# Attention by head pairs: the first head's queries turned feature-major in the bank of the values

## The chip, the cores and the metric

The kernel runs on one core of one Trainium2 chip. The metric is the device time of one execution in microseconds. The core's engines work at the same time, each on its own fixed list of instructions: TensorE (PE, matrix products and transposes; its weight loads are shown apart as PEld), VectorE (DVE), ScalarE (ACT), GpSimd (POOL) and SyncE (SP, which here issues the transfers). An instruction starts when the one ahead of it on its engine lets it and when the semaphores that it waits for have been raised by other engines or by transfers. PE writes its results to PSUM, which this kernel uses as eight banks of 128 rows by 512 floats; ACT and DVE read them from there.

## The reference

Two residual layers over 512 tokens of 1024 features, each followed by a SwiGLU network. The first layer (a state-space mixer beside a gated linear attention) and the networks are outside this change. The second layer is a latent attention with 16 heads; a head has 64 features without position, 32 rotated ones, and 64 value features:

```python
cq, ckv, k_rope = jnp.split(h @ w_dqkv, [MLA_Q_RANK, MLA_Q_RANK + MLA_KV_RANK], axis=-1)   # 384, 256, 32
q = (rms_norm(cq, q_lora_norm) @ w_uq).reshape(bsz, seqlen, H, MLA_NOPE + MLA_ROPE)
q_nope, q_rope = jnp.split(q, [MLA_NOPE], axis=-1)
kv = (rms_norm(ckv, kv_lora_norm) @ w_ukv).reshape(bsz, seqlen, H, MLA_NOPE + MLA_V)
k_nope, v = jnp.split(kv, [MLA_NOPE], axis=-1)
q_nope = rms_norm(q_nope, q_nope_norm)
q_rope = apply_rope(rms_norm(q_rope, q_rope_norm), cos[:, None, :], sin[:, None, :])
k_nope = rms_norm(k_nope, k_nope_norm)
k_rope = apply_rope(rms_norm(k_rope, k_rope_norm), cos, sin)
...
    s = jnp.einsum('bqhd,bkhd->bhqk', qn, k_nope) + jnp.einsum('bqhr,bkr->bhqk', qr, k_rope)
    s = s.astype(jnp.float32) * scale
    p = jax.nn.softmax(jnp.where(mask, s, -jnp.inf), axis=-1).astype(v.dtype)
    return jnp.einsum('bhqk,bkhv->bqhv', p, v)
...
return o @ w_o
```

## The kernel before

**The products.** Weights and activations are split into a high and a low part, and each product is three matmuls (L180 to L182, one after the other in `mm3`): high by high, low by high, high by low. A weight comes by one transfer on SP (`weight`, two buffers); ACT then casts it to its high part (L170, tile `whi`) and DVE subtracts to get the low part (L171, tile `wlo`). What PE made in PSUM and has to be split goes the same way through `split` (ACT's copy at L140, DVE's subtraction at L141).

**The heads.** The attention works by pairs of heads, p = 0 to 7, and by groups of two pairs, g = 0 to 3. Queries and keys of a group are made token-major by the projections (`queries`, `keys`: tiles `qs`, `ks`, and the values `v`), normalised by DVE (`heads_norm`: sums at L1077; factors, whose chain ends with L203 to L206; the factors are applied at L1098 to the keys, L1099 and L1105 to the queries) and rotated in four steps at L993 to L996, of which L996 writes the rotated queries. Then `prepare` turns one pair feature-major: PE transposes the keys of both heads (four transposes, L1127), ACT and DVE (L1141) copy them to `kT`; PE transposes the queries of the first head (four, L1148), ACT copies them to `qT` (L1153); and the same for the second head. L1141 and L1153 carry the gains of the norms, so they are needed anyway.

**A pair's steps.** A pair has three steps (query blocks 0 and 1, block 2, block 3). In each PE makes the scores of both heads (L1181, tile `sco`), DVE masks them and takes the maximum (L1192), ACT the exponential (L1194), DVE the reciprocal (L1196) and the normalisation (L1198); PE transposes the result (L1209, tile `ptr`), and ACT copies it to `pt` (L1218). When all three are there, PE makes the values of both heads (L1228, tile `po`), which `split` turns into operands of the last product (`o_round`, 512 columns at a time).

**The banks.** Of the eight banks, three are the pool `acc`, which hands them out in rotation to all projections, to the transposes of the keys and to those of the queries. The other five belong to this phase by name; `aux(tag)` asks for one:

```python
open_phase(sco=2, ptr=2, po=1, st="sco")
```

A tile that asks for a bank waits until the last reader of its former tile is done. So before the change the bank `po` is used once for each pair, by its values, from the first of their matmuls to the subtraction of `split`.

**The order.** One loop runs over the 24 steps and two more. In step s it emits the values of the pair before (in the second step of a pair), the transposes of the last step's scores, the scores of the next step, and then the pieces that a table, `plan`, gives to that step: projections and norms of later groups, `get_ready(p + 1)`, which is `prepare` for the next pair (in a pair's second step), and the first half of the output product. The order in which the instructions are emitted is not yet the order on the engines. A scheduler puts them there by priority (the order of emission, moved ahead by 90 places for weights and by 150 for some copies), by their data, by a few orders written out by hand, and by its model of when a bank is free. A tile that takes another bank can thus move other instructions on all engines.

Of the kernel before, what the change touches and what calls it, by code (L numbers as in the profile page):

```python
# [46 lines left out]
def kernel(ctx: ExitStack, tc: tile.TileContext, A, yT, stop=99):  # L47
# [11 lines left out]
    def nm(s):  # L59
        cnt[0] += 1  # L60
        return f"{s}_{cnt[0]}"

    def acc():
        return pacc.tile([P, T], F32, tag="acc", name=nm("acc"))
# [11 lines left out]
    def aux(tag="st"):  # L76
        while isinstance(phase["tags"][tag], str):
            tag = phase["tags"][tag]
        return phase["p"].tile([P, T], F32, tag=tag, name=nm(tag), bufs=phase["tags"][tag])
# [19 lines left out]
    ps = acc()  # L99
# [3 lines left out]
    def col(name, i=0, lo=0, hi=P):  # L103
        j = PV[name] + i
        return pv[lo:hi, j:j + 1]
# [18 lines left out]
    def order(i, behind, reason):  # L124

        tc.add_manual_dep(i.ins, behind.ins.name,
                          mybir.DependencyInfo(mybir.DependencyClass.NoSync, mybir.DependencyReason.DATA),
                          reason=reason)
# [229 lines left out]
    with tc.tile_pool(name="gkp", bufs=1) as gkp:  # L358

        ps = aux("a1")  # L360
# [72 lines left out]
        with tc.tile_pool(name="ssd", bufs=2) as sp:  # L433
            cw = sp.tile([P, 60], F32, name="cw", bufs=1)
            j = PV["conv_w"]
# [245 lines left out]
        with tc.tile_pool(name="gla", bufs=2) as gp:  # L681
# [17 lines left out]
            for h in range(4):  # L699
                ps = aux()  # L700
# [209 lines left out]
    with tc.tile_pool(name="mla", bufs=2) as mp, tc.tile_pool(name="mla1", bufs=1) as m1:  # L910
# [30 lines left out]
        ps = acc()  # L941
# [56 lines left out]
        ps = aux()  # L998
# [122 lines left out]
        def prepare(g, hp, mms=None):  # L1121


            qs, ks = pr[g][:2]
            ps = acc()
            for i in range(4):
                tr = E.transpose(ps[:, i * P:(i + 1) * P],  # L1127
                                 ks[:, i, 2 * hp:2 * hp + 2, :].rearrange("p h d -> p (h d)"), ident)
                if mms is not None:
                    order(tr, mms[2][-1], "keys behind products that run until they are normalised")  # L1130
            if mms is not None:
                order(mms[3][0], tr, "the last products behind the keys")
            kts, qts = [], []
            for j in range(2):
                t = kT[(4 * g + 2 * hp + j) % NK]
                kts.append(t)
                with tc.high_priority(offset=FREE):
                    if j == 0 and mms is None:
                        S.activation(t[0:64, :], ps[0:64, :], AF.Copy, scale=col("k_gain", 0, 0, 64))
                    else:  # L1140
                        done = V.tensor_scalar(t[0:64, :], ps[64 * j:64 * j + 64, :],  # L1141
                                               col("k_gain", 0, 64 * j, 64 * j + 64), None, ALU.mult)
            if mms is not None:
                keys.first = done
            for j in range(2):
                ps = acc()
                for i in range(4):
                    tr = E.transpose(ps[0:96, i * P:(i + 1) * P], qs[:, i, 2 * hp + j, :], ident)  # L1148
                    if mms is not None:
                        order(tr, mms[3][0], "queries behind products that run until they are rotated")  # L1150
                qT = mp.tile([96, T], F32, tag="qT", name=nm("qT"), bufs=4)
                with tc.high_priority(offset=FREE):
                    i = S.activation(qT, ps[0:96, :], AF.Copy, scale=col("q_gain", 0, 0, 96))  # L1153
                qts.append(qT)
            if mms is not None:
                order(mms[3][1], tr, "the very last product behind the queries")
                order(keys.last, i, "the last keys behind the first queries")
            return kts, qts
# [107 lines left out]
        ps = aux()  # L1266
# [23 lines left out]
        mms = list(keys(1, wk1))  # L1290
        ahead = [None] * 9
        ahead[0] = prepare(0, 0, mms)
        a0 = apply(0, 1, rq, rk)

# [7 lines left out]
        def get_ready(p):  # L1302
            ahead[p] = prepare(p // 2, p % 2)
            yield
# [132 lines left out]
```

## Time and profile before

| | |
|---|---|
| Median of 3 runs | 1340.86 us (1340.81 to 1341.13) |
| Profiled execution | 1340.57 us |
| Span of its trace | 1338.3 us |
| PE busy between 790 and 965 us, where the pairs are worked off | 173.14 of 175 us |
| DVE busy there | 142.12 us |
| ACT busy there | 131.57 us |
| PE busy in 650 to 790 us, ahead of it | 139.94 of 140 us |
| PE busy in 965 to 1338 us, behind it | 369.46 of 373 us |

The span is the time from the first to the last instruction in the trace; the execution's own time holds a little more on both sides. A busy time is the sum of an engine's instructions without overlap; matmuls are pipelined, so on PE the distance from the start of one row to the start of the next says more than the lengths. The pairs' scores, transposes and values fill the stretch from about 790 to 965 us, with the projections of later pairs and the first half of the output product between them. There PE, DVE and ACT are all near their limits, while ahead of it and behind it PE alone is.

### The profile page before, as it was taken

What the parts mean: (1) busy time and instruction counts of PE and PEld (TensorE: products, weight loads), DVE (VectorE), ACT (ScalarE), POOL (GpSimd) and SP (SyncE); (2) the same over time, 40 slices, a digit from 0 to 9 for tenths busy, and PEclk for the clock granted to TensorE, in tenths of its full rate; (3) what the DMA queues carried; (4) which work ended last, traced back from release to release, by engine and by line L of the source; (5) the groups of instructions that cost most, each with busy time, mean ns of one, the idle gap of its engine ahead of it and who ended that gap; (6) DMA issues with size and microseconds to landing.
All of it is one profiled execution on the core that took longest, in us unless ns stands there. A gap on an engine that the chain in (4) does not pass through costs nothing.

```text
span 1338.3 us, 16696 instructions
## 1 busy us (share of the span) xinstructions
PE 1330.8 (99%) x6508; PEld 1092.8 (82%) x6508; DVE 813.3 (61%) x1389; ACT 561.8 (42%) x956; POOL 7.8 (1%) x35
## 2 busy tenths in 40 slices
PE   9999999999999999999999999999999999999998
PEld 6888888888888888888888888777788888888887
DVE  7889967778976444444333469997674444443221
ACT  7675625444353333222222348986543222232210
POOL 0000000000000000000000000000000000000000
PEclk9999999999999999999999999999999999999999
DMA  5442232312233233333333321110123333333331
GB/s 181 127 142 85 90 95 82 95 63 64 90 97 97 95 95 95 95 96 100 92 102 102 97 92 51 48 32 33 64 95 95 95 96 102 101 95 95 114 112 58
DMA packets 36927, 122.23 MB, mean 91 GB/s; under 512 B 4785, under 2 KB 5809, under 8 KB 36849
## 3 DMA queue, kind: packets, MB, share of 16 engines
q1 hardware_dynamic: 36032, 120.72, 29.2%
q8 instruction: 51, 0.84, 0.3%
q10 hardware_dynamic: 816, 0.46, 0.1%
q14 instruction: 28, 0.22, 0.1%
HBM read 119.03 MB, written 2.13 MB: 91 GB/s over the span
## 4 chain that ended last, share of the span: by engine, by line
PE 92%; DVE 5%; ACT 2%; issue 1%; DMA 1%; SPq 0%; POOL 0%; POOLq 0%; DVEq 0%; ACTq 0%
PE acc L180 28%; PE acc L181 28%; PE acc L182 28%; PE sco L1181 2%; PE po L1228 1%; PE ptr L1209 1%; DVE sc L1192 1%; DVE wlo L171 1%; PE a L570 1%; PE a L810 1%; DVE sc L1198 1%; DVE st L1077 0%; PE a L561 0%; PE a L815 0%; PE a L539 0%
## 5 line engine op out<-in xcount | busy, mean ns | idle before, releaser
L170 ACT CAST whi<-wraw 128x1024 fp32r<-128x1024 f32 (+2 forms) x217 | 223.4, 1030 | 561.6 <-PE acc L181 425.0
L180 PE MATMUL acc<-xh,whi 128*128 128x512 f32 x1144 | 449.8, 393 | 0.2 <-ACT qT L1153 0.2
L181 PE MATMUL acc<-xl,whi 128*128 128x512 f32 x1144 | 446.1, 390 | 0.0
L182 PE MATMUL acc<-xh,wlo 128*128 128x512 f32 x1144 | 445.8, 390 | 0.0
L171 DVE TENSOR_TENSOR wlo<-wraw,whi 128x1024 fp32r<-128x1024 f32 (+2 forms) x217 | 259.2, 1195 | 143.2 <-ACT whi L170 142.7
L180 PEld LDWEIGHTS acc<-xh,whi 128*128 128x128 f32 x1144 | 214.8, 188 | 45.4 <-issue 0.8
L182 PEld LDWEIGHTS acc<-xh,wlo 128*128 128x128 f32 x1144 | 214.8, 188 | 44.5
L181 PEld LDWEIGHTS acc<-xl,whi 128*128 128x128 f32 x1144 | 214.9, 188 | 44.3 <-issue 0.4
L880 DVE TENSOR_TENSOR fu<-acc,R 128x512 f32<-128x512 f32 x44 | 30.4, 691 | 137.4 <-PE acc L182 137.4
L182 PE MATMUL acc<-fhh,wlo 128*128 128x512 f32 x288 | 112.0, 389 | 0.0
L180 PE MATMUL acc<-fhh,whi 128*128 128x512 f32 x288 | 112.0, 389 | 0.0
L181 PE MATMUL acc<-fhl,whi 128*128 128x512 f32 x288 | 112.0, 389 | 0.0
L877 DVE TENSOR_TENSOR fg<-acc,R 128x512 f32<-128x512 f32 x44 | 30.4, 691 | 89.3 <-PE acc L182 89.3
L180 PEld LDWEIGHTS acc<-fhh,whi 128*128 128x128 f32 x288 | 54.1, 188 | 11.3
L182 PEld LDWEIGHTS acc<-fhh,wlo 128*128 128x128 f32 x288 | 54.1, 188 | 11.3
L181 PEld LDWEIGHTS acc<-fhl,whi 128*128 128x128 f32 x288 | 54.1, 188 | 11.1
L180 PE MATMUL acc<-mxh,whi 128*128 128x512 f32 x128 | 49.8, 392 | 0.0
L181 PE MATMUL acc<-mxl,whi 128*128 128x512 f32 x128 | 49.7, 389 | 0.0
L182 PE MATMUL acc<-mxh,wlo 128*128 128x512 f32 x128 | 49.7, 389 | 0.0
L1194 ACT ACTIVATE sc<-sc,mx 128x128 f32<-128x128 f32 (+3 forms) x64 | 35.5, 558 | 12.5 <-DVE mx L1192 12.2
L1181 PE MATMUL sco<-kT,qT 96*128 96x256 f32 (+3 forms) x128 | 39.3, 438 | 0.1
L894 DVE TENSOR_TENSOR x<-x,acc 128x512 f32<-128x512 f32 x16 | 11.0, 688 | 42.9 <-PE acc L182 42.9
(375 smaller groups left out, 1602.3 us busy)
## 6 DMA issues: line engine op xcount, KB each, us to landing
wraw<-in_w_gate_dram SPq DMA_DIRECT2D x44, 512.0 KB, 3.5
wraw<-in_w_up_dram SPq DMA_DIRECT2D x44, 512.0 KB, 3.5
wraw<-in_w_down_dram SPq DMA_DIRECT2D x32, 512.0 KB, 3.6
wraw<-in_w_out_dram SPq DMA_DIRECT2D x16, 512.0 KB, 3.5
wraw<-in_w_down_dram SPq DMA_DIRECT2D x16, 384.0 KB, 3.1
wraw<-in_w_xbc_dram SPq DMA_DIRECT2D x11, 512.0 KB, 3.6
wraw<-in_w_z_dram SPq DMA_DIRECT2D x8, 512.0 KB, 3.5
wraw<-in_w_v_dram SPq DMA_DIRECT2D x8, 512.0 KB, 3.5
```

Of the source, the lines that this page charges most:

```text
L170: cast = S.copy(hi[:, :kc * m], r)
L171: i = V.tensor_tensor(lo[:, :kc * m], r, hi.bitcast(F32)[:, :kc * m], ALU.subtract)
L180: E.matmul(out, ah, bh, start=first, stop=False)
L181: E.matmul(out, ah, bl, start=False, stop=False)
L182: return E.matmul(out, al, bh, start=False, stop=last)
L570: i = E.matmul(pd[64 * h:64 * h + 64, c * P:(c + 1) * P], xdt[:, c, h, :], mt[:, h, c, :], start=True, stop=True)
L810: i = E.matmul(po[e][:, r * P:(r + 1) * P], v[:, r, e * P:(e + 1) * P], sc[:, r, :], start=True, stop=(r == 0))
L877: V.tensor_tensor(g, pg, R, ALU.mult)
L880: V.tensor_tensor(u, pu, R, ALU.mult)
L1181: i = E.matmul(ps[:, at:at + n], self.qts[j][:, b * P:(b + 1) * P], self.kts[j][:, :n], start=True, stop=True)
L1192: V.tensor_tensor_reduce(sc[:, at:at + n], ps[:, at:at + n], am[:, T - n:], -scale, 3e38, ALU.add, ALU.min, mx[:, j:j + 1])
L1194: S.activation(sc[:, at:at + n], sc[:, at:at + n], AF.Exp, bias=mx[:, j:j + 1], scale=-1.0, accum_out=sm[:, j:j + 1])
```

## The change

The first head's four query transposes go to the bank `po`, those of the second head stay in the rotation of `acc`:

```diff
@@ -1143,7 +1143,8 @@ def prepare(g, hp, mms=None):
             for j in range(2):
-                ps = acc()
+
+                ps = acc() if j else aux("po")
                 for i in range(4):
                     tr = E.transpose(ps[0:96, i * P:(i + 1) * P], qs[:, i, 2 * hp + j, :], ident)
```

The file gets one line longer there, so everything behind it is found one line later: L1148 becomes L1149, L1153 L1154, L1181 L1182, L1192 L1193, L1196 L1197, L1198 L1199, L1209 L1210, L1228 L1229. No instruction is added or left out. From the first pair on the scheduler lays the three engines out differently; SP and POOL keep their order. The rows below are an engine's instructions in order: line, operation, result and operands by tile name and number, shape, and how many in a row.

At the third pair (p = 2), PE's list around the transposes of its keys (`ks_6748`) and queries (`qs_6636`) was this. `ptr_7163` and `ptr_7168` are the transposed scores of a step of the pair before, `ptr_7212` of the step after it, `sco_7175` the new pair's first scores:

```order
L1127 MATMUL acc_7142<-ident,ks_6748 128x128 x4
L1209 MATMUL ptr_7163<-ident,sc_7032 128x128 x3
L1209 MATMUL ptr_7168<-ident,sc_7035 128x128 x3
L1148 MATMUL acc_7149<-ident,qs_6636 96x128 x4
L1148 MATMUL acc_7156<-ident,qs_6636 96x128 x4
L1209 MATMUL ptr_7212<-ident,sc_7113 128x128 x4
L1181 MATMUL sco_7175<-kT_6606,qT_7154 128x128
L1181 MATMUL sco_7175<-kT_6606,qT_7154 128x256
```

The second head's score transposes `ptr_7218` stood later, behind a product of six matmuls (`acc_7203`). With the change the same place reads:

```order
L1210 MATMUL ptr_7163<-ident,sc_7032 128x128
L1127 MATMUL acc_7142<-ident,ks_6748 128x128 x4
L1210 MATMUL ptr_7163<-ident,sc_7032 128x128 x2
L1210 MATMUL ptr_7168<-ident,sc_7035 128x128 x3
L1210 MATMUL ptr_7212<-ident,sc_7113 128x128 x4
L1210 MATMUL ptr_7218<-ident,sc_7116 128x128 x4
L1149 MATMUL po_7149<-ident,qs_6636 96x128 x4
L1149 MATMUL acc_7156<-ident,qs_6636 96x128 x4
L180 MATMUL acc_7203<-whi_7062,lh_6455 128x512
L181 MATMUL acc_7203<-wlo_7063,lh_6455 128x512
L1182 MATMUL sco_7175<-kT_6606,qT_7154 128x128
```

Both heads' score transposes moved ahead of the query transposes, and the first two matmuls of the product moved in front of the scores.

On DVE at the same pair, before, with `rt_7128` a half of the rotation of `qs_6636` that L996 adds in, and `kT_6608` the copy of the second head's keys:

```order
L995 TENSOR_TENSOR qs_6636<-rr_7126,csq 128x4x2x32
L1098 TENSOR_TENSOR ks_6748<-ks_6748,hry_7047 128x4x128
L1196 RECIPROCAL sm_7118<-sm_7118 128x2
L996 TENSOR_TENSOR qs_6636<-qs_6636,rt_7128 128x4x2x32
L1198 TENSOR_SCALAR sc_7113<-sc_7113,sm_7118 128x512
L1198 TENSOR_SCALAR sc_7116<-sc_7116,sm_7118 128x512
L1141 TENSOR_SCALAR kT_6608<-acc_7142,pv 64x512
L1099 TENSOR_TENSOR qs_6636<-qs_6636,hry_7047 128x4x2x64
L1105 TENSOR_TENSOR rr_7239<-qs_6636,hry_7047 128x256
```

And with the change:

```order
L1098 TENSOR_TENSOR ks_6748<-ks_6748,hry_7047 128x4x128
L1141 TENSOR_SCALAR kT_6608<-acc_7142,pv 64x512
L1197 RECIPROCAL sm_7118<-sm_7118 128x2
L993 TENSOR_TENSOR rt_7128<-rr_7126,csq 128x8x16
L1199 TENSOR_SCALAR sc_7113<-sc_7113,sm_7118 128x512
L1199 TENSOR_SCALAR sc_7116<-sc_7116,sm_7118 128x512
L994 TENSOR_TENSOR rt_7128<-rr_7126,csq 128x8x16
L995 TENSOR_TENSOR qs_6636<-rr_7126,csq 128x4x2x32
L1099 TENSOR_TENSOR qs_6636<-qs_6636,hry_7047 128x4x2x64
L996 TENSOR_TENSOR qs_6636<-qs_6636,rt_7128 128x4x2x32
```

The key copy, the two normalisations and the L1099 of the pair after now stand ahead of the rotation's last step L996, and the first steps L993 and L994 are pulled apart. A little ahead of it, in the factors of this group (`hry_7047`) and just ahead of the split of the second pair's values, stands a subtraction for a weight that before came 18 rows behind L996:

```order
L203 SCALAR_TENSOR_TENSOR hry_7047<-hrt_7048,hry_7047 128x48
L204 TENSOR_TENSOR hrt_7048<-hry_7047 128x48
L171 TENSOR_TENSOR wlo_7463<-wraw_7460,whi_7462 128x1024
L205 SCALAR_TENSOR_TENSOR hrt_7048<-st_6637,hrt_7048 128x48
L141 TENSOR_TENSOR xl_1269_7096<-po_7086,xh_1268_7095 128x512
L206 SCALAR_TENSOR_TENSOR hry_7047<-hrt_7048,hry_7047 128x48
```

It is the row of `wlo_7463` that moved; the others keep their order.

At the fifth pair (p = 4), PE's list before, with `acc_7549` and `acc_7556` the transposed queries of the two heads:

```order
L1127 MATMUL acc_7542<-ident,ks_7066 128x128 x4
L1148 MATMUL acc_7549<-ident,qs_6852 96x128 x4
L1209 MATMUL ptr_7563<-ident,sc_7432 128x128 x2
L1148 MATMUL acc_7556<-ident,qs_6852 96x128 x4
L1209 MATMUL ptr_7563<-ident,sc_7432 128x128
L1209 MATMUL ptr_7568<-ident,sc_7435 128x128 x3
L1181 MATMUL sco_7575<-kT_6606,qT_7554 128x128
```

With the change:

```order
L1127 MATMUL acc_7542<-ident,ks_7066 128x128 x4
L1149 MATMUL po_7549<-ident,qs_6852 96x128 x4
L1149 MATMUL acc_7556<-ident,qs_6852 96x128 x4
L1210 MATMUL ptr_7563<-ident,sc_7432 128x128 x3
L1210 MATMUL ptr_7568<-ident,sc_7435 128x128 x3
L180 MATMUL acc_7610<-whi_7462,lh_6455 128x512
L1182 MATMUL sco_7575<-kT_6606,qT_7554 128x128
```

The eight query transposes now stand together, directly behind the keys', and a first product matmul stands ahead of the scores. At the second pair the eight query transposes moved ahead of five of six score transposes, and the scores now follow them directly. At the sixth pair the output product `acc_7725` now stands directly behind the query transposes, and the score transposes behind it. At the first pair a matmul of the next queries' product moved ahead of the scores.

## The prediction

> **What bounds the kernel now.** I read the engine totals first, then what TensorE (PE) waits for over the whole span, then the stretches in which the change lies.
>
> ```profile
> PE 1330.8 (99%) x6508; PEld 1092.8 (82%) x6508; DVE 813.3 (61%) x1389; ACT 561.8 (42%) x956; POOL 7.8 (1%) x35
> ...
> PE acc L101 <- DVE idle L98: 1.3, 1, 1.3
> PE acc L1148 <- DVE kT L1141: 0.6, 1, 0.6
> PE acc L1148 <- DVE qs L996: 0.5, 1, 0.5
> PE acc L1148 <- ACT v L1062: 0.4, 1, 0.4
> PE acc L180 <- ACT qT L1153: 0.2, 1, 0.2
> ...
> 800.00:850.00 50.00, 48.94 (x263) 39.50 (x262) 44.33 (x141) 43.73 (x105) 1.73 (x3) 1.00 0.18 58
> 850.00:900.00 50.00, 49.20 (x283) 36.55 (x282) 46.61 (x151) 43.15 (x114) 0.00 (x0) 1.00 0.13 43
> ```
>
> PE is busy for 1330.8 of 1338.3 us: it is the bound, and only 7.5 us of idle time are left in all, most of them at the two ends. The waits (microseconds in total, times, longest) name what can be won in the attention: four short waits of PE, three of them at the query transposes of L1148. Two of these, and the one of L180, are waits for an accumulator bank or can be such; the one for L996 is a wait for data, the rotated queries. The windows (length, then busy time of PE, weight loads, VectorE (DVE), ScalarE (ACT), POOL, then the granted clock) say what stands close behind PE there: between 800 and 900 us DVE is busy 44.3 and 46.6 of 50 us, ACT 43.7 and 43.2. So in this stretch an operation that DVE does earlier makes another one later.
>
> **The gaps that can go.** The PE timeline of before (start, length, line, tile; in brackets the idle time and its releaser) shows them as steps from start to start that are longer than elsewhere. Rows of one place follow each other directly, except that some at 820 and 896 us have other work behind them.
>
> ```profile
> 820.62 0.60 PE L1148 MATMUL acc<-ident,qs 128*96 128x128 f32 x4
> 821.77 0.61 PE L1148 MATMUL acc<-ident,qs 128*96 128x128 f32 x4 [0.56 <-DVE kT L1141]
> ...
> 832.82 0.82 PE L1209 MATMUL ptr<-ident,sc 128*128 128x128 f32 x6
> 834.13 1.08 PE L1148 MATMUL acc<-ident,qs 128*96 128x128 f32 x8 [0.50 <-DVE qs L996]
> ...
> 849.70 0.82 PE L1209 MATMUL ptr<-ident,sc 128*128 128x128 f32 x6
> 850.67 1.08 PE L1148 MATMUL acc<-ident,qs 128*96 128x128 f32 x8
> 851.58 0.60 PE L1209 MATMUL ptr<-ident,sc 128*128 128x128 f32 x4
> 852.08 1.58 PE L1181 MATMUL sco<-kT,qT 96*128 96x128 f32 x8
> ...
> 854.90 0.60 PE L1209 MATMUL ptr<-ident,sc 128*128 128x128 f32 x4
> 855.33 1.46 PE L1181 MATMUL sco<-kT,qT 96*128 96x384 f32 x4
> ...
> 866.62 1.04 PE L1148 MATMUL acc<-ident,qs 128*96 128x128 f32 x8
> 867.50 0.82 PE L1209 MATMUL ptr<-ident,sc 128*128 128x128 f32 x6
> 868.16 1.58 PE L1181 MATMUL sco<-kT,qT 96*128 96x128 f32 x8
> ...
> 883.22 0.38 PE L1209 MATMUL ptr<-ident,sc 128*128 128x128 f32 x2
> 883.96 0.64 PE L1148 MATMUL acc<-ident,qs 128*96 128x128 f32 x4 [0.35 <-ACT v L1062]
> ...
> 896.22 0.82 PE L1209 MATMUL ptr<-ident,sc 128*128 128x128 f32 x6
> 897.27 0.50 PE L180 MATMUL acc<-xh,whi 128*128 128x512 f32 x1 [0.24 <-ACT qT L1153]
> ```
>
> The place at 866 us runs without a wait and gives the measure: eight query transposes take 0.88 us (866.62 to 867.50), so four take 0.44; six score transposes take 0.66, so two take 0.22. Against it the gaps are: (a) at 820 us 1.15 - 0.44 = 0.71; (b) at 832 us 1.31 - 0.66 = 0.65; (c) at 849 us 0.97 - 0.66 = 0.31; (d) at 883 us 0.74 - 0.22 = 0.52; (e) at 896 us 1.05 - 0.66 = 0.39. Sum 2.58 us. This is the most that the change can win if nothing is put in place of them: 0.19% of the time.
>
> **The change part by part.** It adds and removes no operation, no transfer and no byte; DMA issues, SP and POOL keep their order. It takes the first head's four transposes and the copy that reads them (L1153) out of the rotation of the three acc banks and into the po bank. Two kinds of effect follow.
>
> *The bank itself.* The first head's transposes no longer wait for an acc bank but for the split of the values that were in po before, whose last reader is DVE's L141; and each pair's values wait for the copy of the queries. The nearest case of the first in before:
>
> ```profile
> 893.93 0.68 DVE L141 TENSOR_TENSOR xl<-po,xh 128x512 fp32r<-128x512 f32 x1
> ...
> 895.35 1.04 PE L1148 MATMUL acc<-ident,qs 128*96 128x128 f32 x8
> ```
>
> The split ends at 894.61, 0.74 us ahead of the transposes. I cost this new wait at nothing: its cover is the score transposes, scores and key transposes between values and queries, all on PE. If DVE reached the split 1 us later, 0.3 us would show there. Queued behind a waiting transpose on PE is everything, so such a wait would be paid in full. The other way round, the values stand 5 us or more behind the queries' copies. Nothing.
>
> *The order.* With other banks free at other times, the scheduler lays out all three engines anew from the first pair to the fifth; this is the larger part. At (a) the second head's transposes get a bank that ACT has long emptied: the 0.71 goes. At (b) DVE now has the rotation two rows earlier and the 1.12 us split of weights behind it: that wait goes too, though the scores then stand right behind the transposes and wait for ACT's copies, which I put at about the same size.
>
> The third pair (849 to 855 us) decides. There the score transposes of the step before (ptr_7212 and ptr_7218, eight) now stand ahead of the query transposes, and on DVE five operations that stood behind the rotation of these queries (the first L996 shown) stand ahead of it: the weight split wlo_7463, the key copy kT_6608, two normalisations L1198, and a L1099. Their steps in before:
>
> ```profile
> 850.21 0.40 DVE L996 TENSOR_TENSOR qs<-qs,rt 128x256 f32<-128x256 f32 x1
> 850.53 0.88 DVE L1198 TENSOR_SCALAR sc<-sc,sm 128x512 f32<-128x512 f32 x2
> 851.44 0.76 DVE L1141 TENSOR_SCALAR kT<-acc,pv 64x512 f32<-64x512 f32 x1
> 852.23 0.69 DVE L1099 TENSOR_TENSOR qs<-qs,hry 128x512 f32<-128x512 f32 x1
> 852.84 0.42 DVE L1105 TENSOR_TENSOR rr<-qs,hry 128x256 f32<-128x256 f32 x1
> ...
> 855.22 1.21 DVE L171 TENSOR_TENSOR wlo<-wraw,whi 128x1024 fp32r<-128x1024 f32 x1
> 856.34 0.48 DVE L1198 TENSOR_SCALAR sc<-sc,sm 128x128 f32<-128x128 f32 x2
> ```
>
> From start to start: 0.91 for the two normalisations, 0.79 for the key copy, 0.61 for L1099, 1.12 for the weight split: 3.43 us. DVE is full here, so nothing that PE wins at (a) and (b) lets DVE come to this point earlier; the rotation ended at 850.61 and PE's queries began at 850.67, so they now begin near 850.67 + 3.43 = 854.10. Of that wait PE does eight score transposes that it did later in before: 0.50 us (851.58 to 852.08) and 0.43 us (854.90 to 855.33). What is left at the scores of 855.33 is 3.43 - 0.50 - 0.43 = **2.50 us later**, and it holds whatever was won up to there: (a), (b) and (c) are swallowed, since the time of this point is DVE's.
>
> The bounds of this term: nothing, if DVE has enough air from other rows to be back in time; and about 3.1, if the split wlo_7463 has to wait for its cast. The cast is ACT's:
>
> ```profile
> 844.24 1.06 ACT L170 CAST whi<-wraw 128x1024 fp32r<-128x1024 f32 x1
> ...
> 844.84 0.21 DVE L205 SCALAR_TENSOR_TENSOR hrt<-st,hrt 128x48 f32<-128x48 f32 x1
> ```
>
> The split now stands where L205 began at 844.84, and the cast ended at 845.30: up to about 0.5 us of waiting, against some tenths saved because short dependent rows of the factors now have other work between them. I take 2.50, the value nearest to the rows, with no correction.
>
> Behind this point I find no second place of the kind: the later rotations and key copies keep 0.4 us or more in front of PE's need. What is left of the gaps goes: at (d) both heads' transposes find free banks (0.52), at (e) the product that waited for ACT's copy takes a bank emptied long before (0.39). I credit both in full, less nothing: 0.91. Bounds: 0 and 1.1.
>
> **The sum** against the profiled execution: 1340.57 + 2.50 - 0.91 = 1342.16 us (its span is 1338.3, with 2.3 us around it, which stay). The median of the runs of before, 1340.86, stands 0.29 above that execution; so the forecast median is 1342.16 + 0.29 = 1342.45, rounded to **1342.4 us**, 0.12% above. A measurement of this kernel tells about 0.2%, 2.7 us, from no change.
>
> **The rivals.** *The gaps go and nothing takes their place.* For it: DVE's share of 1338 us is only 61%, and if the five operations find air, PE gets all of 2.58: 1340.86 - 2.58 = 1338.3. Against it: DVE's 46.6 of 50 us in just this window, and the rows that follow each other without a break. Even then the change is at the edge of what can be measured. Chance 9%, a third of it beyond 0.2%.
>
> *The banks were not what PE waited for* (the waits named are by the last semaphore), the new order costs and wins little: 1340.9, within half a microsecond. For it: two of the five gaps are waits for data. Against it: the order shown changes anyway. 12%.
>
> *Slower: PE's clock falls at the third pair.* PE would now stand still ahead of ptr_7212: it comes there at about 850.36 - 0.71 = 849.65 and is released when the two normalisations are done, near 852.5, so it idles some 2.8 us, does 0.9 us of work and idles again till 854.1. The longest wait of PE in before is 1.3 us. What PE does after standing still shows only at the start:
>
> ```profile
> 1.32 4.45 PE L101 MATMUL acc<-idle 128*128 128x512 bf16 x10 [1.32 <-DVE idle L98]
> 5.29 0.90 PE L363 MATMUL a<-xh,whi 128*48 128x512 f32 x1
> ...
> 7.54 0.40 PE L363 MATMUL a<-xh,whi 128*48 128x512 f32 x1
> 7.77 0.39 PE L364 MATMUL a<-xh,wlo 128*48 128x512 f32 x1
> ```
>
> The first ten matmuls of 512 columns took (5.29 - 1.32) / 10 = 0.40 us each, later ones 0.23 from start to start: 1.7 us lost on ten, and I add 0.6, a third of it, for those behind them, the first of which is still 0.90 long. Priced like that the time is 1342.4 + 2.3 = 1344.7. It decides from the point where the idle stretch is long enough; the granted clock in the windows (1.00 throughout) has no such stretch to show it by. Chance 13%. [...]
>
> *The values' split is late in each pair.* If DVE came to L141 a microsecond late behind its other rows, seven pairs would pay a few tenths each, 2 us on top: 1344.4. Against it: in the order the split stands ahead of the score rows as before. 4%.
>
> **How the numbers follow.** The forecast has what is left, 62%; its own range, by the bounds of its two terms (0 to 3.1 and 0 to 1.1, not both at their ends), is 1340.6 to 1343.8, and a tenth of it lies above 1343.5. The range that should hold 8 times in 10 reaches down over the case of the banks and part of the way to that of the gaps, and up to the clock: 1339.4 to 1344.8. Faster by over 0.2% (below 1338.2): 0.03. Slower (above 1343.5): 0.06 of the forecast, 0.13 and 0.04: 0.23. Within 0.2%: 0.74.
>
> **What the profile of the changed kernel would show.** If I am right, PE has a new wait of 2 to 3 us near 849 to 852 us at the score transposes L1210, released by DVE's normalisation L1199, and a second one below 1 us at the query transposes L1149, released by L996; the waits for kT and for v at the query transposes are gone, and none of po's transposes waits for L141. PE's idle time in 800 to 900 us rises from 1.9 us to about 4. Wrong would be: the queries of the third pair beginning before 852 us (the order then costs less than its rows say), waits of over 1 us at any other pair, or matmuls of 0.4 us from start to start behind 854 us.

## The result and the profile after

The changed kernel takes 1342.81 us (median of 20 runs, 1341.65 to 1344.28) against 1340.89 us of the kernel before (20 runs, 1340.27 to 1342.91 and a single one of 1471.93): 1.92 us more, a ratio of 1.0014 with a 95% interval of 1.0007 to 1.0020. It is slower, since the interval lies above 1, but by less than the 0.2% that the prediction took as its bound. The profiled execution took 1343.48 us, its span is 1341.3 us.

The changed kernel's waits of PE (total, times, longest) and its two windows of 50 us (length; busy PE, weight loads, DVE, ACT, POOL; granted clock; DMA share, GB/s):

```profile
PE ptr L1210 <- DVE sc L1199: 2.9, 1, 2.9
PE acc L101 <- DVE idle L98: 1.3, 1, 1.3
...
800.00:850.00 50.00, 50.00 (x269) 40.60 (x268) 44.26 (x138) 43.12 (x103) 1.73 (x3) 1.00 0.23 75
850.00:900.00 50.00, 47.14 (x266) 35.50 (x264) 44.30 (x146) 41.00 (x109) 0.00 (x0) 0.97 0.10 32
```

The four waits in the attention are gone; the stretch from 800 to 850 us has no idle time left (1.06 us before). In their place stands one wait of 2.9 us behind 850 us, and the granted clock of that window is 0.97, where it was 1.00 in both before.

To see where time was won and lost, the same rows are compared in both traces. The first pair here is the last row ahead of the pairs (L1268 before, L1269 after); then the values of the first, second, third, fourth and fifth pair (L1228 before, L1229 after). First before, then after:

```profile
804.74 0.60 PE L1268 MATMUL sco<-ident,kro 128*32 128x128 f32 x4
...
843.14 2.38 PE L1228 MATMUL po<-pt,v 128*64 128x512 f32 x16
859.87 2.37 PE L1228 MATMUL po<-pt,v 128*64 128x512 f32 x16
876.22 2.37 PE L1228 MATMUL po<-pt,v 128*64 128x512 f32 x16
890.17 2.38 PE L1228 MATMUL po<-pt,v 128*64 128x512 f32 x16
909.18 2.37 PE L1228 MATMUL po<-pt,v 128*64 128x512 f32 x16
```

```profile
805.78 0.60 PE L1269 MATMUL sco<-ident,kro 128*32 128x128 f32 x4
...
842.95 2.38 PE L1229 MATMUL po<-pt,v 128*64 128x512 f32 x16
863.88 2.38 PE L1229 MATMUL po<-pt,v 128*64 128x512 f32 x16
880.35 2.38 PE L1229 MATMUL po<-pt,v 128*64 128x512 f32 x16
893.64 2.37 PE L1229 MATMUL po<-pt,v 128*64 128x512 f32 x16
912.17 2.37 PE L1229 MATMUL po<-pt,v 128*64 128x512 f32 x16
```

The profiled execution of after is already 1.04 us late when it reaches the pairs, at work that the change doesn't touch. That belongs to the executions: after's stands 0.67 us above its kernel's median and before's 0.32 below, 0.99 together. So it is taken off below, and likewise in every kernel of the experiments (-0.19 to 1.20 us at the same row). The differences then are -1.23 us at the first values, +2.97 at the second, +3.09, +2.43 and +1.95 at the next. So 1.23 us were won up to the third pair's preparation, 4.20 lost there, 0.12 more lost at the fourth pair, 0.66 and 0.48 won at the next two. The sum, 1.95 us, agrees with the medians' 1.92.

The loss, on PE and DVE of the changed kernel at the third pair (start, length):

```profile
849.63 0.71 PE L1210 MATMUL ptr<-ident,sc 128*128 128x128 f32 x5
853.19 1.83 PE L1210 MATMUL ptr<-ident,sc 128*128 128x128 f32 x8 [2.86 <-DVE sc L1199]
854.82 1.06 PE L1149 MATMUL po<-ident,qs 128*96 128x128 f32 x4
855.67 1.06 PE L1149 MATMUL acc<-ident,qs 128*96 128x128 f32 x4
856.38 0.64 PE L180 MATMUL acc<-whi,lh 128*128 128x512 f32 x1
```

```profile
845.67 1.22 DVE L171 TENSOR_TENSOR wlo<-wraw,whi 128x1024 fp32r<-128x1024 f32 x1
...
851.12 0.76 DVE L1141 TENSOR_SCALAR kT<-acc,pv 64x512 f32<-64x512 f32 x1
...
852.17 0.88 DVE L1199 TENSOR_SCALAR sc<-sc,sm 128x512 f32<-128x512 f32 x2
...
854.11 0.42 DVE L996 TENSOR_TENSOR qs<-qs,rt 128x256 f32<-128x256 f32 x1
```

PE is out of work at 850.34, and waits for the two normalisations; then its eight score transposes take 1.63 us from start to start (0.20 each, where eight transposes took 0.88 before), the next four 0.85 and the last four 0.71. Windows of one microsecond of the same kernel show why:

```profile
851.00:852.00 1.00, 0.00 (x0) 0.00 (x0) 0.94 (x4) 1.00 (x4) 0.00 (x0) 1.00 0.00 0
852.00:853.00 1.00, 0.00 (x0) 0.00 (x0) 1.00 (x5) 0.13 (x1) 0.00 (x0) 1.00 0.00 0
853.00:854.00 1.00, 0.81 (x5) 0.84 (x6) 1.00 (x4) 0.00 (x0) 0.00 (x0) 0.66 0.00 0
854.00:855.00 1.00, 1.00 (x6) 0.99 (x5) 1.00 (x4) 0.59 (x1) 0.00 (x0) 0.50 0.06 16
855.00:856.00 1.00, 1.00 (x7) 0.95 (x6) 1.00 (x4) 0.67 (x2) 0.00 (x0) 0.50 0.00 0
856.00:857.00 1.00, 1.00 (x6) 0.94 (x5) 1.00 (x3) 0.83 (x2) 0.00 (x0) 0.63 0.00 0
```

The granted clock, the third number from the end of each row, fell to a half when PE had just begun to work again. From these shares (twice 0.34 + 0.50 + 0.50 + 0.37) it was low for 3.42 us.

### The profile page after: what moved, and what is told of

The parts are those of the page before. It is cut to its first block, busy times and chain, and to the rows that moved or that the text cites. A ratio compares the mean times of both kernels' runs of the same rounds, so it can differ in the third digit from the quotient of the medians.

```text
span 1341.3 us, 16692 instructions
## 1 busy us (share of the span) xinstructions
PE 1331.9 (99%) x6508; PEld 1094.5 (82%) x6508; DVE 813.5 (61%) x1389; ACT 562.1 (42%) x956; POOL 7.8 (1%) x35
## 4 chain that ended last, share of the span: by engine, by line
PE 95%; ACT 2%; DVE 2%; issue 1%; DMA 0%; POOL 0%; SPq 0%; POOLq 0%; ACTq 0%
PE acc L180 28%; PE acc L181 28%; PE acc L182 28%; PE sco L1182 2%; PE po L1229 1%; PE ptr L1210 1%; PE a L570 1%; PE a L810 1%; ACT sc L1195 0%; PE a L561 0%; PE a L815 0%; PE a L539 0%; DMA x<-in_xT_dram 0%; DVE wlo L171 0%; ACT whi L170 0%
## 5 line engine op out<-in xcount | busy, mean ns | idle before, releaser
L1182 PE MATMUL sco<-kT,qT 96*128 96x256 f32 (+3 forms) x128 | 39.1, 438 | 0.0
```

What stands on the lines that cost most here:

```text
L1182: i = E.matmul(ps[:, at:at + n], self.qts[j][:, b * P:(b + 1) * P], self.kts[j][:, :n], start=True, stop=True)
```

## The experiments

The theory: the bank itself costs nothing; the loss is DVE's rows that now stand ahead of the rotation, the wait of PE that follows, and the clock's fall after that wait. The rivals: the hand-over of the bank po costs something at every pair; the slow matmuls have another cause; the gaps that went come back elsewhere. Each kernel was timed against before on the same chip, with 11 runs of its own and 21 or 33 of before.

**The weight's subtraction back behind the rotation.** The kernel has a list `hold`: a weight's subtraction that is emitted while something stands in it is ordered behind that.

```diff
         def keys(g, wkv=None):
 
+            if g == 3:
+                hold.append(q_done[1, 0])
             wkv = wkv or k_weights(g)
+            hold.clear()
```

> The change, and besides one order by hand: DVE's subtraction of the last keys' weight (wlo_7463), which the change had moved ahead, stays behind the rotation of the third pair's queries. Theory A (the moved rows on DVE and the order on PE that follows from them are the loss; the bank itself costs nothing): the query transposes of the third pair begin at most 0.5 us later than before, PE waits there 1 to 2 us, the granted clock stays 1.000, and the gaps at the other pairs stay closed: 1339.5 to 1340.5 us. Theory B (the hand-over of the bank po is the loss, the order only its form): still 1342.5 or more. Theory C (the change wins nothing anywhere, the gaps come back elsewhere): 1340.9.

Measured: 1340.31 us (1340.02 to 1341.59), ratio 0.9996 (0.9987 to 1.0005). With that one row back, the scheduler also puts the query transposes ahead of the score transposes again. PE at the third pair of this kernel:

```profile
849.08 0.82 PE L1213 MATMUL ptr<-ident,sc 128*128 128x128 f32 x6
851.86 0.64 PE L1152 MATMUL po<-ident,qs 128*96 128x128 f32 x4 [1.97 <-DVE qs L996]
```

This execution was 0.61 us late at the last row ahead of the pairs (805.35), so the queries begin 851.86 - 0.61 - 850.67 = 0.58 us later than before, as against 3.11 with the change (854.82 - 1.04 - 850.67), and slightly more than the 0.5 expected. What PE had won up to here it spends in a wait of 1.97 us, since the rotation on DVE is not earlier. Theory B falls: the bank is used as in the change, and the time is 2.5 us lower. Theory C is not settled by this time alone, since its interval contains 1; the pair of kernels with and without po further down settles it.

**Work for PE in the wait.** Twenty transposes of the unit matrix are put into po ahead of the third pair's queries:

```diff
                 ps = acc() if j else aux("po")
+                if (g, hp, j) == (1, 0, 0):
+                    for _ in range(20):
+                        E.transpose(ps[:, 0:P], ident, ident)
```

> The change, and besides 20 idle transposes of the unit matrix into the third pair's po bank ahead of its queries, 20 x 0.11 = 2.2 us of PE work that lies in the 2.86 us wait; nothing of the result changes. Theory A1 (PE's clock fell because of the wait, and that costs about 1.0 us): the granted clock is 1.000, the eight score transposes take 0.87 us instead of 1.63, the wait before them is about 0.7 us, and the time falls to about 1341.8. Theory A2 (the slow matmuls behind the wait come from something else that stands in this place): they stay at about 0.2 us each and the time stays at 1342.8. Theory A3 (the idle work delays the path): above 1343.

Measured: 1342.11 us (1341.62 to 1343.30), ratio 1.0011 (1.0002 to 1.0020). The PE timeline of this kernel:

```profile
849.80 2.24 PE L1150 MATMUL po<-ident 128*128 128x128 f32 x19
851.87 0.82 PE L1213 MATMUL ptr<-ident,sc 128*128 128x128 f32 x6
853.37 1.06 PE L1213 MATMUL ptr<-ident,sc 128*128 128x128 f32 x8 [0.68 <-ACT pt L1222]
854.75 0.64 PE L1152 MATMUL po<-ident,qs 128*96 128x128 f32 x4 [0.32 <-DVE qs L996]
```

With more work on PE than the change has, the loss is smaller: the score transposes are back at 0.13 us or less each, the granted clock is 1.00 throughout, and the wait for the rotation that I had expected behind them comes out, 0.32 us. (The 0.68 us are named after ACT's copy, which ended at 853.26; DVE's second normalisation had ended at 853.22.) The second pair's values, at 863.06 and with 1.20 us of lateness ahead of the pairs taken off, stand 1.99 us after before's, 0.98 less than with the change. By the medians it is 0.70 us less; the two intervals overlap, so the size rests on the trace.

**The change for some of the pairs.** Once for p = 0 and 1 alone, once for p = 3 to 7:

```diff
-                ps = acc() if j else aux("po")
+                ps = aux("po") if not j and 2 * g + hp < 2 else acc()
```

```diff
-                ps = acc() if j else aux("po")
+                ps = aux("po") if not j and 2 * g + hp >= 3 else acc()
```

> The change for the first two pairs alone, all others in the three acc banks as before. Theory A: the order at the third pair is that of the change though its own queries are not in po, with PE's wait of nearly 3 us and the clock's fall; the gaps at the fifth and sixth pair (0.9 to 1.0 us together) are back: about 1343.8. Theory B (each pair in po costs something): two pairs of eight, 1341.4 at most, and no wait over 1 us at the third pair.

> The change for the last five pairs alone (p = 3 to 7), the first three in acc as before. Theory A: the first three pairs run as before, with their gaps, the third pair as before without the long wait; the gaps at the fifth and sixth pair are gone, 0.9 to 1.0 us: about 1339.9. Theory B: five pairs of eight pay for the bank, 1341.5 to 1342. Theory C (gaps closed there come back behind): 1340.9.

Measured: 1343.78 us (ratio 1.0018, 1.0009 to 1.0027) with the first two pairs, 1340.26 us (0.9994, 0.9986 to 1.0003) with the last five. In the first, the third pair has its queries in acc and still shows `PE ptr L1210 <- DVE sc L1199` with 2.9 us and the clock's fall: the loss at the third pair comes from the order that the first two pairs' banks bring about. The sum of both, +2.89 and -0.63 us against the same runs of before, is +2.26; the whole change has +1.92. The last five pairs win less than the 0.9 to 1.0 us expected, and the interval of their time contains 1; by the trace, the values of the fourth pair stand 0.16 us and those of the fifth 0.66 us earlier than before's. At the fifth pair the gap came back in part as a new wait of 0.40 us of the scores for ACT's copy, as theory C has it.

**The key copy back, the weight's subtraction left where it is.**

```diff
             if mms is not None:
                 keys.first = done
+            if (g, hp) == (1, 0):
+                order(done, q_done[1, 0], "copy of the keys behind the rotation")
```

> The change, and besides one order by hand: DVE's copy of the second head's keys at the third pair (kT_6608, 0.78 us) stays behind the rotation; the weight's subtraction stays where the change put it, and PE's order is that of the change. If each row on DVE counts in full, PE's wait at the score transposes shrinks from 2.86 to about 2.1 us; whether the clock falls after 2.1 us is open: with the fall 1342.0, without it about 1341.0 and a granted clock of 1.000. Rival (the wait is not set by DVE's rows but by PE's own order): wait still 2.9 us and 1342.8.

Measured: 1342.18 us (1340.76 to 1342.92), ratio 1.0007 (0.9998 to 1.0015). The wait is 2.38 us, 0.48 less than with the change, where the full row would have been 0.78. Part of the row's place is taken: a rotation step, L994, now stands ahead of the normalisations with 0.19 us, and their reciprocal waits 0.16 us for ACT's exponential. The 11 runs fall into two groups by the mean granted clock that comes with each: five at 1.000 take 1340.76 to 1341.50 us (median 1341.20), six at 0.999 take 1342.18 to 1342.92 (median 1342.58). The profiled execution is of the second group:

```profile
850.18 0.17 DVE L1199 RECIPROCAL sm<-sm 128x2 f32<-128x2 f32 x1 [0.16 <-ACT sc L1197]
...
851.47 1.07 PE L1212 MATMUL ptr<-ident,sc 128*128 128x128 f32 x8 [2.38 <-DVE sc L1201]
...
852.00:853.00 1.00, 0.89 (x8) 0.65 (x7) 0.97 (x3) 0.86 (x2) 0.00 (x0) 0.98 0.07 16
853.00:854.00 1.00, 1.00 (x7) 0.93 (x6) 0.97 (x3) 0.67 (x2) 0.00 (x0) 0.50 0.00 0
854.00:855.00 1.00, 1.00 (x4) 0.81 (x3) 1.00 (x4) 0.83 (x2) 0.00 (x0) 0.50 0.00 0
855.00:856.00 1.00, 1.00 (x5) 0.90 (x4) 0.18 (x1) 0.07 (x1) 0.00 (x0) 0.50 0.00 0
```

PE is at work again from 851.47 on, at full clock for about 1.5 us, and then the clock falls. So after 2.4 us of standing still the fall comes in about half of the executions, as far as the mean clock and the gap between the two groups' times tell (one execution was profiled), and it costs 1.4 us between the groups' medians. This answers both of the times that I had given, 1342.0 and 1341.0.

**The rotation first.** On top of the weight's order of the first experiment, the third pair's L1098 to L996 get a priority 150 places ahead:

```diff
+            with tc.high_priority(offset=FREE if (g, hp) == (1, 0) else 0):
-            k_done[g, hp] = V.tensor_tensor(ks, ks, ...)
-            i = V.tensor_tensor(qs[:, :, :, 0:64], ...)
+                k_done[g, hp] = V.tensor_tensor(ks, ks, ...)
+                i = V.tensor_tensor(qs[:, :, :, 0:64], ...)
...
+            with tc.high_priority(offset=FREE if (g, hp) == (1, 0) else 0):
-            i = V.tensor_tensor(rr, qs[:, :, :, 64:96], ...)
+                i = V.tensor_tensor(rr, qs[:, :, :, 64:96], ...)
...
+            with tc.high_priority(offset=FREE if (g, hp) == (1, 0) else 0):
-            q_done[g, hp] = rope(...)
+                q_done[g, hp] = rope(...)
```

> The change, and besides: the weight's subtraction behind the rotation of the third pair, and the rows that make this pair's keys and rotated queries (L1098 to L996 in the change's lines) moved ahead by 150 places in the scheduler's priorities. On DVE the rotation then follows the split of the values after eight rows. If DVE's rows ahead of the rotation are all of the loss, PE's wait at the third pair is 0.3 to 0.8 us (1.97 with the subtraction alone put back) and the time is 1338.6 to 1339.5, below both kernels. Rival (the scores' maximum and normalisation, now later, are wanted next): a wait of 1 us or more at the score transposes L1216 and 1340 to 1341.

Measured: 1339.13 us (1338.63 to 1339.56), ratio 0.9985 (0.9977 to 0.9994); once more beside the next experiment, 1339.11 us, 0.9986 (0.9977 to 0.9995). PE's wait at the third pair is down to 0.39 us:

```profile
850.26 0.64 PE L1155 MATMUL po<-ident,qs 128*96 128x128 f32 x4 [0.39 <-DVE qs L996]
```

This is faster than both kernels, by 1.8 and 3.7 us. The scores' normalisation, which is later in it, is not missed: no wait of 1 us stands in the attention. One wait for the bank itself does show in it. At the sixth pair the scheduler puts the second head's transposes first, and the weight load of po's stands until the split of the values:

```profile
894.35 0.60 PE L1155 MATMUL acc<-ident,qs 128*96 128x128 f32 x4
...
895.01 0.39 PEld L1155 LDWEIGHTS po<-ident,qs 128*96 128x96 f32 x4 [0.32 <-DVE xl L141]
```

On PE po's transposes begin at 895.02, 0.67 us after the others began, where four take 0.44: 0.23 us lost there, in the second profiled execution of this kernel as well.

**The same without the change.** All queries in acc, with the edits of the last experiment; and that experiment again:

> The kernel before (both heads in the acc banks) with only the edits of e6_rotation_first, none of the change. If the gaps at the banks are what the change wins (1.0 us at the fifth and sixth pair, 1.2 us up to the third), this kernel keeps the gaps named after kT and v at the query transposes, 1.0 us or more, and takes 1340.0 to 1340.9, about that of the kernel before. Rival (the order of e6 is all of its gain and the bank po adds nothing): 1339.1 as e6.

> e6_rotation_first once more, on the same chip and against the same runs of before as e9: 1338.9 to 1339.4, and below e9 by 0.7 us or more if the bank po has a gain of its own; within 0.4 us of e9 if not.

Measured: 1340.81 us (ratio 0.9999, 0.9991 to 1.0008) and 1339.11 us. Without po the gaps are where they were before; the waits of PE in the kernel without it:

```profile
PE acc L1155 <- DVE kT L1147: 0.6, 1, 0.6
PE acc L1155 <- DVE qs L996: 0.5, 1, 0.5
PE acc L180 <- ACT qT L1160: 0.2, 1, 0.2
```

So the order alone wins nothing and the bank alone loses 1.9 us, while both together win 1.8: the bank po, with the order that the scheduler makes of it, is worth 1.70 us as soon as the third pair's rotation is on time. The slowest of the 11 runs with po took 1339.73 us, the fastest without it 1340.56. By the traces, 1.23 us of the difference stand at the first pair's values, 1.19 at the second's and 1.79 at the fifth's: what is won ahead of the third pair is kept there.

**Both heads, and the other head.** `ps = aux("po")` for both heads, and `ps = aux("po") if j else acc()`:

> Both heads' query transposes in po, so that the second head must wait for ScalarE's copy of the first: a real wait for the bank, which the change has not. Theory A (a bank wait is paid where no other work stands between the two): in the order of this kernel most pairs have two to ten matmuls between them, the copy takes 0.68 us and some 0.3 us to start, so 0.2 to 0.8 us at each of eight pairs: 1342 to 1346, and the waits are named at L1149 after L1154. Rival (the other work covers it): 1340 to 1341.5.

> The second head's transposes in po, the first head's in acc: the other head, with the same order of rows as the change on DVE and at the third pair on PE. Theory A (order is all): as the change, 1342.4 to 1343.2, with a wait of 2.9 us at the third pair and the clock's fall. Theory B (the first head's wait for the values' split matters): faster by 0.5 us or more than the change.

Measured: 1340.21 us (ratio 0.9994, 0.9985 to 1.0003) with both heads, a miss of theory A there. PE's matmuls show no wait at L1149 for L1154, its weight loads show five short ones, 1.6 us together (`PEld po L1149 <- ACT qT L1154: 1.6, 5, 0.4`). Weight loads overlap the matmuls (in before the two are busy 1092.8 and 1330.8 of 1338.3 us), and the steps of PE ahead of these transposes are longer than elsewhere by 0.1 us or less each. So the wait is there and mostly covered; the scheduler puts other work between, at the third pair nine product matmuls, the first and the last of which are shown with the two heads' transposes:

```profile
852.17 0.64 PE L1149 MATMUL po<-ident,qs 128*96 128x128 f32 x4
...
852.68 0.42 PE L180 MATMUL acc<-whi,lh 128*128 128x384 f32 x1
...
854.16 0.34 PE L182 MATMUL acc<-xh,ll 128*128 128x384 f32 x1
854.34 0.60 PE L1149 MATMUL po<-ident,qs 128*96 128x128 f32 x4
```

In that kernel the rotation also comes out earlier than with the change, so it is no test of the bank by itself. The other head takes 1342.85 us (1.0014, 1.0005 to 1.0023), as the change, with the same wait of 2.9 us: which head's transposes wait for the values' split makes no difference.

## Why the prediction was right, and where it was not

The direction, the place and the size were right: 1342.4 us forecast, 1342.81 measured, the loss at the third pair. The size is in part an accident of two errors.

- **The third pair's 2.50 us** were measured as 2.97 us (863.88 - 1.04 - 859.87), made of two parts. The rotation came 854.11 - 1.04 - 850.21 = 2.86 us later, not 3.43: between the dependent steps of the factors, DVE now has other work in place of short stalls, which I had named as "some tenths" and left out. The eight rows L198 to L206, each counted to the start of DVE's next row, take 1.68 us before and 1.31 after; this is 0.37 of the 0.57 us, and the rest is spread over other short waits. With 0.93 us of score transposes taken off, as in the prediction, that would have been 1.93 us; the run with work in the wait, at full clock, shows 1.99.
- **The clock's fall** was a rival with 13%, and the forecast had none of it. It happened in the profiled execution and, by the mean clock, in up to 18 of 20 runs (the two at 1.000 are the two fastest, 1341.65 and 1342.06 us); it adds 0.98 us by the traces, not the 2.3 that I took from the start of the kernel. The profile gives a granted clock of 1.00 for that start too, in each microsecond from 0 to 10, so the slow matmuls there are no measured fall. Which idle stretch is long enough the rival left open; in the attention, waits of up to 1.97 us came without a fall, one of 2.38 us with a fall in its profiled execution and, by the runs' times, in about half of the runs. The 1.00 given for before's windows holds for those shown; from 1338.0 us to its end at 1338.3, behind the last matmul, the trace has 0.52. The idle stretch given as the reason for the fall, PE standing still for about 2.8 us ahead of ptr_7212, came out with 2.86; that it fits so closely is luck. With the 1.04 us taken off, PE stopped at 849.29 (849.65 forecast, which has gap (a) taken off but not (b)) and was released at 852.15 (near 852.5 forecast), so two errors of about 0.35 us cancel.
- **The gaps (a) to (c)** went and were swallowed, as forecast. At (a) and (b) 1.23 us were won of the 1.36 that the two gaps add up to, more than the prediction's 849.65 allows for: it had the scores give (b) back in a wait for ACT's copies, and that wait did not come. All of it was spent waiting at the third pair, because the rotation on DVE does not come earlier. The kernel with the weight's row back shows the same: 1.97 us of wait where before had none of that size.
- **The gaps (d) and (e)** brought 0.66 + 0.48 = 1.14 us, forecast 0.91; 0.12 of it had been lost at the fourth pair, where the prediction found nothing.
- **The bank itself** costs nothing in the changed kernel, as costed: po's transposes wait for no split in its trace. At the sixth pair, the nearest case, the split ends at 897.47 + 0.69 = 898.16 and the transposes begin at 898.82: 0.66 us to spare, 0.74 in the prediction. The price is not nothing in every order: the rotation-first kernel pays 0.23 us at this pair, and the one with both heads in po waits for the split there too (its weight load stands 0.5 us for L141).
- **The other rivals.** That the banks were not what PE waited for is refuted by the pair of kernels whose sources differ in the bank alone, 1340.81 and 1339.11 us. That the gaps go and nothing takes their place came true only with the rotation moved ahead: 1339.1, where the rival had 1338.3. A late split of the values was not seen in the changed kernel, and in the rotation-first kernel only at the one pair named.
- **The second wait**, below 1 us at L1149 for L996, did not show in the changed kernel: the slow score transposes ended at 854.82, after the rotation. At full clock it is there, with 0.32 us. For the same reason the idle time in 800 to 900 us is 2.86 us instead of about 4.

What stays open: why the scheduler moved the weight's subtraction. That it follows from the first two pairs' banks is shown by the kernel with these alone; by which step of its model was not traced.

## What to carry to other kernels

A freed bank won what its gaps showed only as far as the next point that another engine times: in 800 to 900 us, where before's DVE is busy for 44.3 and 46.6 of 50 us, the 1.23 us won ahead of such a point turned into a wait there. Before dropping an edit that moves a scheduler's order, look for the one row that moved against you; here an order by hand for two chains of DVE turned +1.9 us into -1.8. And a wait of TensorE cost more than its length here: behind waits of 2.38 to 2.9 us the granted clock stood at 0.50 for 3.41 to 3.42 us, in about half of the runs or more as far as their times and mean clocks tell, which cost another 1.0 to 1.4 us.

## What the runs showed of the hardware

In the attention the clock's fall came with the longer waits, and by the runs' times not in every execution of one kernel. None of the profiled executions whose longest wait is 1.97 us or less shows it, all four with 2.38 us or more do (the change, its first two pairs alone, the key copy back, the other head). In the kernel with 2.38 us the runs' times fall into two groups of five and six, 1.4 us apart. The mean clock alone is a rough sign, since 0.999 also comes with four of 11 runs of the rotation-first kernel, whose longest wait in the attention is 0.39 us. The two profiled executions of that kernel show why: the clock falls at the end of the span, behind the last matmul, where PE has no work left. Of these falls the one that comes soonest behind the last matmul is in the kernel with the last five pairs alone (the last matmul, then windows of one microsecond):

```profile
1333.88 0.39 PE L182 MATMUL acc<-fhh,wlo 128*128 128x512 f32 x1
...
1336.00:1337.00 1.00, 0.00 (x0) 0.00 (x0) 0.00 (x0) 0.00 (x0) 0.00 (x0) 0.65 0.57 217
1337.00:1338.00 1.00, 0.00 (x0) 0.00 (x0) 0.00 (x0) 0.00 (x0) 0.00 (x0) 0.50 0.00 0
```

Here PE stopped at 1334.27 and the clock fell at 1336.3, 2.0 us later; in before it fell 3.6 us after the last matmul, and with the weight's row back it had not fallen after 3.8 us, when the span ended. So in these profiles no single length of standing still marks the fall.

When the clock falls behind a wait in the attention, it does so 0.1 us (the change: 853.19 to about 853.3) to 1.8 us (the other head: 852.52 to about 854.3) after the work has begun again, stays at 0.50 for 3.41 to 3.42 us in all four, and costs 1.0 to 1.4 us here. Idle work on TensorE, 2.2 us of transposes that nobody reads, kept the clock up in its profile; the second pair's values came 0.98 us earlier than with the change, while the medians, 0.70 us apart, have intervals that overlap.
